# SwiGLU on one core: the first store split over two queues by even and odd partitions, tile 0 computed whole

## The chip, the cores and the metric

The kernel runs on one core of one Trainium2 chip. The metric is the device time of one execution in microseconds (us), as the median of several executions. Five engines work beside each other on a core; this kernel uses ScalarE (ACT in the profile) for the gate, VectorE (DVE) for the product, and SyncE (SP), ScalarE and GpSimd (POOL) to issue transfers. The transfers themselves are carried out by 16 DMA engines, which all three issuing queues share. Two of those queues, SP's and ACT's, are called hardware_dynamic in the profile (q1 and q10), and GpSimd's is called software_dynamic (q0).

## The reference

x is a float32 array of 8192 x 8192. Each row is cut into a left half a and a right half b, and the output is an 8192 x 4096 array:

```
a, b = np.split(x, 2, axis=-1)
silu_b = b / (1 + np.exp(-b))
return a * silu_b
```

So 268.4 MB are read, 134.2 MB are written, and there are two element-wise steps between.

## The kernel before

The 8192 rows are cut into 33 tiles. Tiles 0 and 32 hold 128 rows, one to each of the 128 partitions. Tiles 1 to 31 hold 256 rows, two consecutive rows to each partition. One row of x is 32 KB and one row of the output 16 KB, so a partition's part of a big tile is 64 KB in the load and 32 KB in the store, and in tiles 0 and 32 it is half of that.

There are three buffers in SBUF, slot 0 to 2; tile i lies in slot i % 3. Four things happen to a tile, all in its slot:

- `load(i)` (line 48) issues the load from SP. It waits until the store of tile i - 3, which read the same slot, has landed. Tile 31 (`apart`) is loaded in two halves, one for each row of a partition.
- `swiglu` (lines 57 and 59) runs the gate Silu on ACT in place over b, and then the product on DVE, which writes a * silu(b) packed to the front of the slot. A big tile is one gate and one product. Tile 0 is done in two column halves of 2048 each, two gates and two products, and tile 31 in two halves after its two loads.
- `store(i, engine)` (line 66) issues one store of the whole tile after its last product. The stores of tiles 0 to 29 go out from ACT, but those of tiles 3, 17 and 19 from GpSimd. The stores of tiles 30, 31 and 32 go out from SP.

The order on each engine is the order of the calls in the program (`manual_schedule`): loads 0, 1 and 2 first, and then for each tile gate, product, store and the load of tile i + 3. The instructions of one engine are issued in this order, and a waiting instruction holds up all behind it on its engine. On ACT the store of a tile stands ahead of the gate of the next tile. On SP there are only loads until the last three stores. `behind` records which instruction a new one has to wait for; it takes the list of targets as arguments.

Of the kernel before, what the change touches and what calls it, by code (L numbers as in the profile page):

```python
# [1 line left out]

# [4 lines left out]

_SILU = mybir.ActivationFunctionType.Silu


@with_exitstack
def kernel(
    ctx: ExitStack,
    tc: tile.TileContext,
    x: bass.AP,
    out: bass.AP,
):
    nc = tc.nc
    N, M = x.shape  # L20
    half = M // 2
    P = nc.NUM_PARTITIONS
    rows = [1] + [2] * (N // (2 * P) - 1) + [1]
    first = [P * sum(rows[:i]) for i in range(len(rows))]
    last = len(rows) - 1
    apart = last - 1

    pool = ctx.enter_context(tc.tile_pool(name="sbuf", bufs=1))
    ctx.enter_context(tc.manual_schedule())
    slots = [pool.tile([P, 2 * M], x.dtype, name=f"slot{s}") for s in range(3)]  # L30
    touched = [[] for _ in slots]
    newest = {}
    landed, made, stored = {}, {}, {}

    def behind(inst, s, *targets):
        for t in touched[s]:
            if t not in targets and t is not newest.get(inst.ins.engine):
                tc.declare_no_dep(inst.ins, t.ins, reason="ordered by the other waits")
        touched[s].append(inst)
        newest[inst.ins.engine] = inst  # L40
        return inst

    def load(i):
        s, r = i % 3, rows[i]
        src = x[first[i] : first[i] + P * r].rearrange("(p r) m -> p (r m)", r=r)
        cuts = [0, M, r * M] if i == apart else [0, r * M]
        for c0, c1 in zip(cuts, cuts[1:]):
            inst = nc.sync.dma_start(out=slots[s][:, c0:c1], in_=src[:, c0:c1])  # L48
            behind(inst, s, *([stored[i - 3]] if i >= 3 and c0 == 0 else []))
            landed.setdefault(i, []).append(inst)  # L50

    def swiglu(i, k0, k1, c0, c1):
        s, r = i % 3, rows[i]
        v = slots[s][:, : r * M].rearrange("p (k s c) -> p k s c", k=r, s=2)
        to = slots[s][:, : r * half].rearrange("p (k c) -> p k c", k=r)
        b = v[:, k0:k1, 1, c0:c1]
        gate = nc.scalar.activation(out=b, in_=b, func=_SILU)  # L57
        behind(gate, s, landed[i][min(k0, len(landed[i]) - 1)])
        prod = nc.vector.tensor_mul(out=to[:, k0:k1, c0:c1], in0=v[:, k0:k1, 0, c0:c1], in1=b)  # L59
        behind(prod, s, gate, *([made[i]] if i in made else []))  # L60
        made[i] = prod

    def store(i, engine):
        s, r = i % 3, rows[i]
        dst = out[first[i] : first[i] + P * r].rearrange("(p r) m -> p (r m)", r=r)
        inst = engine.dma_start(out=dst, in_=slots[s][:, : r * half])  # L66
        behind(inst, s, made[i])
        stored[i] = inst

    for i in range(3):  # L70
        load(i)
    for i in range(last + 1):
        if i == 0:
            swiglu(i, 0, 1, 0, half // 2)
            swiglu(i, 0, 1, half // 2, half)
        elif i == apart:
            swiglu(i, 0, 1, 0, half)
            swiglu(i, 1, 2, 0, half)
        else:
            swiglu(i, 0, rows[i], 0, half)  # L80
        if i < last - 2:
            store(i, nc.gpsimd if i in (3, 17, 19) else nc.scalar)
            load(i + 3)
        else:
            store(i, nc.sync)


# [1 line left out]
_INS = ['x']  # L89
_OUTS = [((8192, 4096), 'float32')]  # L90


# [23 lines left out]
```

## Time and profile before

| what | value |
|---|---|
| time, median of 3 runs | 935.28 us (935.13 to 935.88) |
| the profiled execution, its own time | 935.16 us |
| its span in the profile | 933.4 us |
| DVE busy, ACT busy | 278.5 us (30%), 226.7 us (24%) |
| bytes moved by the DMA engines | 402.67 MB, mean 431 GB/s |
| gate of 128x8192, 128x4096, 128x2048, mean | 7029, 3616, 1901 ns |
| product of 128x8192, 128x4096, 128x2048, mean | 8693, 4426, 2288 ns |

The profile describes one execution on the chip. Its page gives the busy time of each engine, the busy share of the DMA engines in slices of the span, the DMA queues with their packets and bytes, the chain of work that ended last, the costliest groups of instructions, and the DMA issues with the median time from issue to landing. The trace behind the page answers further questions: the instructions of a stretch in order of time, the waits, or the busy time and the GB/s of chosen stretches. The 1.76 us between the span (933.4) and the time of that execution (935.16) lie outside of what the profile covers.

### The profile page before, as it was taken

Reading aid. Unit: us, or ns where it says so; the run is one execution under the profiler, and the core shown is the slowest. Engines: PE = TensorE matmul, PEld = TensorE weight load, DVE = VectorE, ACT = ScalarE, POOL = GpSimd, SP = SyncE. Lnnn points to the kernel's source line nnn. Section 1 sums busy time; section 2 is a strip of 40 time slices with the busy share of each in tenths; the row PEclk is TensorE's granted clock in tenths of the full one; section 3 lists DMA queues with packets and bytes.
Section 4 is the critical chain, followed back from the end, with each engine's and each line's share of the span. In section 5 each row is a group of like instructions: output and inputs, shape, how many; then the busy total and the mean of one; then the engine's idle time right before and its main releaser. Section 6 shows DMA issues by size and latency. Waiting matters only on the chain.

```text
span 933.4 us, 211 instructions
## 1 busy us (share of the span) xinstructions
DVE 278.5 (30%) x35; ACT 226.7 (24%) x36; POOL 1.9 (0%) x7
## 2 busy tenths in 40 slices
DVE  1131333123331233312333113332133321333241
ACT  2332033311333203332033320233202333023330
POOL 0000000000000000000000000000000000000000
DMA  9999999999999999999999999999999999999999
GB/s 404 404 458 418 427 452 441 410 445 428 445 427 434 442 411 447 430 435 435 440 420 441 438 424 445 427 454 425 424 452 407 448 427 429 448 441 413 431 438 389
DMA packets 9650, 402.67 MB, mean 431 GB/s; under 512 B 1073, under 2 KB 1073, under 8 KB 1073
## 3 DMA queue, kind: packets, MB, share of 16 engines
q1 hardware_dynamic: 5328, 278.92, 69.1%
q10 hardware_dynamic: 3888, 111.15, 27.6%
q0 software_dynamic: 432, 12.58, 3.1%
q14 instruction: 2, 0.01, 0.0%
HBM read 268.44 MB, written 134.22 MB: 431 GB/s over the span
## 4 chain that ended last, share of the span: by engine, by line
DMA 78%; DVE 11%; ACT 9%; another core or an unknown queue 1%; issue 0%; SPq 0%; ACTq 0%
DMA slot<-in_x_dram 42%; DMA out_dram<-slot 36%; DVE slot L59 11%; ACT slot L57 9%; SPq L48 0%; ACTq L66 0%
## 5 line engine op out<-in xcount | busy, mean ns | idle before, releaser
L59 DVE TENSOR_TENSOR slot<-slot 128x8192 f32<-128x8192 f32 (+2 forms) x35 | 278.5, 7961 | 637.9 <-ACT slot L57 637.9
L57 ACT ACTIVATE slot<-slot 128x8192 f32<-128x8192 f32 (+2 forms) x35 | 225.4, 6444 | 684.5 <-DMA slot<-in_x_dram 684.5
L66 POOL DMA_DIRECT2D out_dram<-slot x3 | 1.7, 578 | 568.7 <-DVE slot L59 568.7
L57 ACT ACT_TABLE_LOAD x1 | 1.3, 1283 | 0.7 <-PEq L100 0.7
L100 POOL MEMSET const-bfloat16-1.0<- 128x1 bf16 x1 | 0.1, 102 | 0.0
L100 POOL MEMSET const-float32-0.0<- 128x1 f32 x1 | 0.1, 99 | 0.2 <-issue 0.2
L100 POOL MEMSET const-float32-1.0<- 128x1 f32 x1 | 0.1, 99 | 0.0
L100 POOL MEMSET const-uint8-127<- 128x1 uint8 x1 | 0.1, 99 | 0.0
## 6 DMA issues: line engine op xcount, KB each, us to landing
out_dram<-slot ACTq DMA_DIRECT2D x26, 4096.0 KB, 33.5
slot<-in_x_dram SPq DMA_DIRECT2D x4, 4096.0 KB, 23.5
out_dram<-slot POOLq DMA_DIRECT2D x3, 4096.0 KB, 34.2
out_dram<-slot SPq DMA_DIRECT2D x2, 4096.0 KB, 25.0
out_dram<-slot ACTq DMA_DIRECT2D x1, 2048.0 KB, 28.1
out_dram<-slot SPq DMA_DIRECT2D x1, 2048.0 KB, 16.1
slot<-in_x_dram SPq DMA_DIRECT2D x30, 37.6
```

The costliest lines, as they stand in the source:

```text
L57: gate = nc.scalar.activation(out=b, in_=b, func=_SILU)
L59: prod = nc.vector.tensor_mul(out=to[:, k0:k1, c0:c1], in0=v[:, k0:k1, 0, c0:c1], in1=b)
L66: inst = engine.dma_start(out=dst, in_=slots[s][:, : r * half])
L100: nc = _bacc.Bacc("TRN2", target_bir_lowering=False, num_devices=1)
```

## The change

Two things are changed. Tile 0 loses its special case: it is gated and multiplied by one instruction each (128x4096) in place of two (128x2048). And `store` takes several engines: with n engines, the tile's partitions are dealt out in turn, so that with two the first engine issues a store of the even partitions and the second one of the odd partitions (64 rows each). Only the store of tile 0 uses this, with ACT for the even and GpSimd for the odd partitions. As a tile can now have two stores, `stored[i]` is a list, and the load of tile 3 waits for both. With one engine, `store` issues the same transfer as before.

```diff
-            behind(inst, s, *([stored[i - 3]] if i >= 3 and c0 == 0 else []))
+            behind(inst, s, *(stored[i - 3] if i >= 3 and c0 == 0 else []))
...
-    def store(i, engine):
-        s, r = i % 3, rows[i]
-        dst = out[first[i] : first[i] + P * r].rearrange("(p r) m -> p (r m)", r=r)
-        inst = engine.dma_start(out=dst, in_=slots[s][:, : r * half])
-        behind(inst, s, made[i])
-        stored[i] = inst
+    def store(i, *engines):
+        s, r, n = i % 3, rows[i], len(engines)
+        dst = out[first[i] : first[i] + P * r].rearrange("(q n r) m -> n q (r m)", n=n, r=r)
+        parts = slots[s][:, : r * half].rearrange("(q n) c -> n q c", n=n)
+        for j, engine in enumerate(engines):
+            inst = engine.dma_start(out=dst[j], in_=parts[j])
+            behind(inst, s, made[i])
+            stored.setdefault(i, []).append(inst)
...
-        if i == 0:
-            swiglu(i, 0, 1, 0, half // 2)
-            swiglu(i, 0, 1, half // 2, half)
-        elif i == apart:
+        if i == apart:
             swiglu(i, 0, 1, 0, half)
             swiglu(i, 1, 2, 0, half)
         else:
             swiglu(i, 0, rows[i], 0, half)
-        if i < last - 2:
+        if i == 0:
+            store(i, nc.scalar, nc.gpsimd)
+            load(i + 3)
+        elif i < last - 2:
             store(i, nc.gpsimd if i in (3, 17, 19) else nc.scalar)
             load(i + 3)
```

On the engines: ACT has one gate in place of two ahead of its first store, and that store has 64 rows in place of 128. DVE has one product in place of two. GpSimd's queue gets a store of 64 rows ahead of its store of tile 3. SP's list is the same, but its fourth load waits for two transfers. Everything after that is unchanged.

## The prediction

> **What bounds the kernel now.** I read the page's engine rows first, then its DMA rows and queues.
>
> ```profile
> span 933.4 us, 211 instructions
> ...
> DVE 278.5 (30%) x35; ACT 226.7 (24%) x36; POOL 1.9 (0%) x7
> ...
> DMA  9999999999999999999999999999999999999999
> ...
> q1 hardware_dynamic: 5328, 278.92, 69.1%
> q10 hardware_dynamic: 3888, 111.15, 27.6%
> q0 software_dynamic: 432, 12.58, 3.1%
> ```
>
> No compute engine is busy a third of the time. The DMA row has a 9 in every slice, and the queues' shares add up to 99.8% of 16 DMA engines over the whole span. So the transfers are the bound. Where could there still be idle time? The table of stretches of 87 us (three tiles each; columns: busy time of DVE, ACT, POOL, clock, DMA share, GB/s) shows it:
>
> ```profile
> 0.00:87.00 87.00, 21.88 (x4) 19.05 (x5) 0.20 (x4) 1.00 0.99 421
> 87.00:174.00 87.00, 26.08 (x3) 21.09 (x3) 0.67 (x1) 1.00 1.00 434
> ...
> 435.00:522.00 87.00, 26.08 (x3) 21.09 (x3) 0.53 (x1) 1.00 1.00 435
> ...
> 870.00:933.40 63.40, 21.97 (x4) 17.88 (x4) 0.00 (x0) 1.00 0.96 413
> ```
>
> All nine stretches between 87 and 870 us stand at 434 or 435 GB/s, with a store from GpSimd in them (three) or without. Against 434, the first stretch lacks 87 x 13/434 = 2.6 us and the last 63.4 x 21/434 = 3.1 us. The first is the start of the first load: issued at 0.74, its 4.19 MB land 12.3 us later where 434 GB/s would need 9.7, so 2.6 us again. Nothing else is left of the first stretch, which is the one that the change edits.
>
> Then the timeline and the chain of waits, for what stands around the first store.
>
> ```profile
> 13.09 3.71 ACT L57 ACTIVATE slot<-slot 128x2048 f32<-128x2048 f32 x2 [11.08 <-DMA slot<-in_x_dram]
> 15.04 4.49 DVE L59 TENSOR_TENSOR slot<-slot 128x2048 f32<-128x2048 f32 x2 [15.04 <-ACT slot L57]
> 19.56 0.38 ACTq L66 DMA_DIRECT2D out_dram<-slot  x1
> 35.63 7.03 ACT L57 ACTIVATE slot<-slot 128x8192 f32<-128x8192 f32 x1 [18.83 <-DMA slot<-in_x_dram]
> 42.69 8.69 DVE L59 TENSOR_TENSOR slot<-slot 128x8192 f32<-128x8192 f32 x1 [23.16 <-ACT slot L57]
> 51.42 0.34 ACTq L66 DMA_DIRECT2D out_dram<-slot  x1
> 58.77 7.03 ACT L57 ACTIVATE slot<-slot 128x8192 f32<-128x8192 f32 x1 [16.11 <-DMA slot<-in_x_dram]
> ```
>
> Gates begin when their loads have landed, so the first three loads land at 13.1, 35.6 and 58.7. The first store is issued at 19.56. The DMA issues put its landing 28.1 us later, and SP issues load 3 at 47.66, which is the same moment.
>
> ```profile
> out_dram<-slot ACTq DMA_DIRECT2D x1, 2048.0 KB, 28.1
> ```
>
> **Why a 2 MB store takes 28.1 us.** The packet counts fit one packet per partition row and 16 small ones per transfer: ACT's 27 stores x (128 + 16) = 3888. So a packet of load 1 or 2 has 64 KB and one of store 0 has 16 KB. If the queues take turns packet by packet, store 0 gets 16/(64 + 16) = 1/5 of 434 GB/s, or 87, and its 2.10 MB take 24.1 us; with the 2.6 us of start and landing from above, 26.7, against 28.1 measured. With equal shares in bytes it would be 12.3. The row decides for turns by packets. [...]
>
> **The change, part by part.**
>
> Tile 0 whole: one gate (3.62) in place of two (3.71), one product (4.43) in place of two (4.49), but now one behind the other. The store is issued at 13.09 + 3.62 + 0.02 + 4.43 + 0.02 = 21.18, which is 1.62 us later than 19.56. ACT's next gate waits for load 1 until beyond 35 and DVE until 42, so nobody on these engines is held up.
>
> Store 0 on two queues: two issues of 64 packets in place of one of 128, at 0.38 us on ACT and 0.67 on GpSimd (its first issue at 103.75, 0.31 us after the product ended; 0.53 later). GpSimd has nothing else before tile 3. If GpSimd's queue has a turn of its own, store 0 gets 32/(64 + 16 + 16) = 1/3 of 434, or 145 GB/s: 14.5 us and 2.6 to 4.0 of start and landing, so it lands at 38 to 40 in place of 47.7, and SP issues load 3 there, once both halves are in.
>
> What that earlier load 3 is worth: nothing, by the order on SP. Load 2 stands ahead of it in the same queue and lands at 58.7. And a share that store 0 gains is one that loads 1 and 2 lose. Load 1: from 13.1 alone until store 0's packets begin (some 2.0 after its issue: 23.2) 4.4 MB, the remaining 4.0 MB at 2/3 of 434 in 13.8 us: 37.0. (The same working for before gives 35.1, the row 35.6.) So load 1 lands near 37.5, 1.9 us later, and store 1 follows at 53.3. Load 2 has the engines almost alone from 38 to 55 and lands near 57.8, 0.9 us earlier.
>
> Is anything late next? Load 4 waits for store 1, issued 1.9 us later, and in before SP issued it at 83.95, when load 3 had 3.7 us to go (87.66). After, it is issued near 85.9, when load 3 has about 0.9 to go. The loads' queue then runs dry for some 2 us, but store 2 (issued near 73.6, 4.19 MB) has the engines meanwhile. What one queue leaves, the other takes; loads 1 and 2 (16.8 MB, 38.7 us) and the stores behind them leave no moment without packets. The 1.6 us is hidden by that, and if that cover were gone it would cost 1.6 at most.
>
> The end: a shift of 1 to 3 us comes to load 32, which waits for store 29 (issued at 885.95, while the loads of tile 31 land until 898.6), and to the last store, issued at 916.4, when store 31, issued at 906.7, has 4.19 MB or 9.7 us to move behind store 30. I estimate 9 us of slack in both places.
>
> The sum: bytes the same, packets the same but 16 more small ones, GpSimd's queue at the same 434 GB/s, idle time the same 2.6 and 3.1 us. One price is not shown by any row: a transfer of every other partition. Each of before uses all 128. At 434/16 = 27.1 GB/s per engine a packet of 16 KB takes 0.605 us, and store 0 has 8 per engine. Between 0 (each engine keeps to its part of SBUF) and each of these packets taking twice as long, +4.8 us; below nothing there is no room, since the engines have no idle time to win. I take 0, since all rows, with loads and stores of 16, 32 and 64 KB packets and one to three queues, stand at 434; both ends go into the range. So 933.4 + 0 in span, 935.16 + 0 in time; beside the median of 935.28 I say **935.3**.
>
> **The rivals.**
>
> [...]
>
> *A shift that opens a gap: slower.* If the phases moved by over 9 us, load 32 or store 32 would come late and the gate and product of the last tile (3.62 + 4.43) would stand open: up to 8 us, 943. My shift is 1 to 3 us.
>
> *The earlier load 3 pays: faster.* It would have to fill idle time of the first stretch, which has 2.6 us, all of it before the first landing. At the very most 935.2 - 2.6 = 932.6.
>
> *The change does not do what it says.* If the second queue gets no turn of its own, store 0 lands near 49 and load 3 is issued there, still ahead of load 2's end: 935.3.
>
> **How the numbers follow.** Hidden by a full queue, at no price: 0.55. No turn of its own, same time: 0.05. Collision: 0.32, of which 0.29 over 0.2% and 0.03 under. A gap: 0.05. The earlier load 3 pays: 0.03. About 0.2% is what a measurement of this kernel can tell from no change. So faster 0.03, same 0.55 + 0.05 + 0.03 = 0.63, slower 0.29 + 0.05 = 0.34. The likeliest case alone would be 934.6 to 936.2; with the collision's full price the range is 934.6 to 940.1.
>
> **What would show it.** Right: one gate and one product for tile 0, store issues near 21.2, both halves landed by 40, load 3 issued there, tile 1's gate near 37.5, tile 2's near 57.8, and 87:870 still at 434. [...] Wrong by a gap: a low rate in the last 30 us alone.

## The result and the profile after

The changed kernel takes 937.89 us (median of 10 runs, 936.73 to 938.37), beside 935.24 us for the kernel before in the same comparison (10 runs). The ratio is 1.0022, with a 95% interval of 1.0012 to 1.0032. It is slower by 0.2%, at the edge of what the prediction counted as no change, and 2.6 us above the 935.3 that the likeliest case gave. Single runs of the kernel before lie above 936 as well, 9 of the 111 in all comparisons of this document. The profiled execution took 937.18 us with a span of 935.4; that is 2.0 us more span than before.

The page and the table of stretches of 87 us of the changed kernel (the same columns as before):

```profile
span 935.4 us, 211 instructions
...
DVE 278.5 (30%) x34; ACT 226.6 (24%) x35; POOL 2.5 (0%) x8
...
q1 hardware_dynamic: 5328, 278.92, 69.1%
q10 hardware_dynamic: 3824, 110.10, 27.3%
q0 software_dynamic: 512, 13.63, 3.4%
```

```profile
0.00:87.00 87.00, 21.81 (x3) 18.96 (x4) 0.84 (x5) 1.00 0.99 418
87.00:174.00 87.00, 26.08 (x3) 21.09 (x3) 0.55 (x1) 1.00 1.02 432
...
522.00:609.00 87.00, 26.08 (x3) 21.09 (x3) 0.53 (x1) 1.00 1.00 434
...
870.00:935.40 65.40, 21.97 (x4) 17.88 (x4) 0.00 (x0) 1.00 0.96 413
```

The sums of work are as before, and so is the end. Look at the second line: the DMA engines are busier (1.02 for 1.00) and move less (432 for 434). From 174 us on the table stands at 434 again, but for 430 between 435 and 522; there the busy share is 0.99, and no packet took longer than usual.

The timeline shows each step of the start:

```profile
13.13 3.62 ACT L57 ACTIVATE slot<-slot 128x4096 f32<-128x4096 f32 x1 [11.11 <-DMA slot<-in_x_dram]
...
21.23 0.56 ACTq L68 DMA_DIRECT2D out_dram<-slot  x1
21.51 0.64 POOL L68 DMA_DIRECT2D out_dram<-slot  x1 [21.07 <-DVE slot L59]
37.37 7.03 ACT L57 ACTIVATE slot<-slot 128x8192 f32<-128x8192 f32 x1 [20.62 <-DMA slot<-in_x_dram]
...
53.16 0.36 ACTq L68 DMA_DIRECT2D out_dram<-slot  x1
58.98 7.03 ACT L57 ACTIVATE slot<-slot 128x8192 f32<-128x8192 f32 x1 [14.58 <-DMA slot<-in_x_dram]
...
88.04 7.03 ACT L57 ACTIVATE slot<-slot 128x8192 f32<-128x8192 f32 x1 [22.04 <-DMA slot<-in_x_dram]
...
122.63 7.03 ACT L57 ACTIVATE slot<-slot 128x8192 f32<-128x8192 f32 x1 [27.56 <-DMA slot<-in_x_dram]
```

Loads 1 and 2 land at 37.4 and 59.0, store 1 goes out at 53.16. The gate of tile 4 starts at 122.63; before it started here:

```profile
119.15 7.03 ACT L57 ACTIVATE slot<-slot 128x8192 f32<-128x8192 f32 x1 [24.44 <-DMA slot<-in_x_dram]
```

And this is when SP issues load 4, first before, then after:

```profile
83.95 0.33 SPq L48 DMA_DIRECT2D slot<-in_x_dram  x1
```

```profile
86.89 0.33 SPq L48 DMA_DIRECT2D slot<-in_x_dram  x1
```

After, the last packet of load 3 ends between 84.5 and 86.5 on the 16 engines, so none of them had a load packet left when load 4 was issued at 86.89. (Load 3 counts as landed on them some 1.5 us later, between 86.1 and 88.0.) The stretch of 90 to 100 us, when load 4's first packets run, first before, then after:

```profile
90.00:100.00 10.00, 5.25 (x1) 4.71 (x1) 0.00 (x0) 1.00 1.09 472
```

```profile
90.00:100.00 10.00, 4.90 (x1) 5.07 (x1) 0.00 (x0) 1.00 1.01 370
```

GB/s by itself jumps in so short a stretch (before: 472 from 90 to 100 us, 410 from 88.5 to 100). GB/s over the DMA share does not: 472/1.09 = 433 and 410/0.95 = 432 before, 370/1.01 = 366 from 90 to 100 us after. Busy engines moved less.

**Where the 2 us lie.** The trace has a record of every packet with its start, its length and its queue. Nearly all packets of a size take the same time in both kernels: 0.611 us for 16 KB, 1.213 for 32 KB, 2.418 for 64 KB. So each packet's extra time can be read off. Summed and divided by 16 engines it is 1.48 us per engine before and 3.33 after, 1.85 more, beside 2.0 of span. Before it is spent at the first packets of the kernel (0.58) and where store 0 joins (20 to 35 us: 0.82). After there are 0.56 and 0.92 in these places, 0.24 between 55 and 85, and 1.58 between 90 and 100, nearly all of it (1.46) on the first or second packet of load 4 on each engine (up to 3.93 us for a packet of 64 KB).

### The profile page after: what moved, and what is told of

It is laid out like the page before. It is cut to its first block, busy times and chain, and to the rows that moved or that the text cites. A ratio compares the mean times of both kernels' runs of the same rounds, so it can differ in the third digit from the quotient of the medians.

```text
span 935.4 us, 211 instructions
## 1 busy us (share of the span) xinstructions
DVE 278.5 (30%) x34; ACT 226.6 (24%) x35; POOL 2.5 (0%) x8
## 4 chain that ended last, share of the span: by engine, by line
DMA 78%; DVE 11%; ACT 9%; another core or an unknown queue 1%; issue 0%; SPq 0%; ACTq 0%
DMA slot<-in_x_dram 42%; DMA out_dram<-slot 35%; DVE slot L59 11%; ACT slot L57 9%; SPq L48 0%; ACTq L68 0%
## 5 line engine op out<-in xcount | busy, mean ns | idle before, releaser
L59 DVE TENSOR_TENSOR slot<-slot 128x8192 f32<-128x8192 f32 (+1 forms) x34 | 278.5, 8190 | 640.0 <-ACT slot L57 640.0
L57 ACT ACTIVATE slot<-slot 128x8192 f32<-128x8192 f32 (+1 forms) x34 | 225.3, 6628 | 686.6 <-DMA slot<-in_x_dram 686.6
## 6 DMA issues: line engine op xcount, KB each, us to landing
out_dram<-slot ACTq DMA_DIRECT2D x1, 1024.0 KB, 19.6
out_dram<-slot POOLq DMA_DIRECT2D x1, 1024.0 KB, 19.4
slot<-in_x_dram SPq DMA_DIRECT2D x30, 37.5
```

## The experiments

All kernels were timed in five rounds against the kernel before, and the ratio is given with its 95% interval. Three theories were written down before the first runs. D: a load that comes into a load queue that has run dry costs. G: the half stores themselves cost. S: the later store costs.

**One part at a time.** `e1` keeps tile 0's two column halves and takes the two-queue store; `e2` takes the whole tile 0 and leaves the store on ScalarE:

```diff
 e1
-        if i == apart:
+        if i == 0:
+            swiglu(i, 0, 1, 0, half // 2)
+            swiglu(i, 0, 1, half // 2, half)
+        elif i == apart:
 e2
-            store(i, nc.scalar, nc.gpsimd)
+            store(i, nc.scalar)
```

> The two-queue store alone; tile 0 stays in two column halves. Theory D (the loss is load 4 coming into a load queue that has run dry, because store 0's larger share delays load 1 and so store 1): load 1 lands near 37.3, SP issues load 4 near 86.8, and the time is 1.5 to 3 us above before. Theory G (the half stores themselves cost: a third queue, or rows two partitions apart): also 1.5 to 3 us above. Theory S (the store that is issued 1.6 us later costs): as before, 935.2.

> Tile 0 whole alone; store 0 goes out from ScalarE in one piece. Theory D: store 0 keeps its fifth, load 1 lands near 35.1, load 4 is issued by 84 and the queue never dries: 935.2 within 0.5. Theory G: 935.2. Theory S: 1.5 to 3 us above before.

Measured: e1 936.84 us, 1.0016 (1.0007 to 1.0025); e2 936.88 us, 1.0017 (1.0008 to 1.0026). Each part alone costs 1.7 us, both together 2.6. e1 went as D and G said: load 1 at 37.84, load 4 issued at 86.40, extra packet time of 1.32 us per engine near 90. e2's time is what S expected (1.5 to 3 us above before) and not what D did; yet D's late load is there: load 1 landed at 37.24, not at 35.1, and load 4 was issued late after all:

```profile
86.65 0.33 SPq L48 DMA_DIRECT2D slot<-in_x_dram  x1
```

But in e2 only 0.23 us per engine was lost there. How a smaller loss gives the same time is answered below.

**The same queue, and load 4 in time.** `e3` issues both half stores from ScalarE; `e4` is the changed kernel with tile 1 in two halves, so that store 1 goes out earlier:

```diff
 e3
-            store(i, nc.scalar, nc.gpsimd)
+            store(i, nc.scalar, nc.scalar)
 e4
-        if i == apart:
+        if i in (1, apart):
```

> Tile 0 whole and the two half stores kept, but both on ScalarE's queue, one after the other. Theory D: one queue, one turn, store 0 keeps its fifth and lands near 49; load 4 is in time: 935.2 to 935.7. Theory G by rows two partitions apart: 1.5 to 3 us above before. Theory G by a third queue: 935.2.

> The changed kernel with tile 1 gated and multiplied in two halves (one row of a partition each), so that its store goes out 3.2 us sooner. Theory D: store 1 near 49.9, load 4 issued near 83.6, before load 3 is through, and the loss is gone: 935.2 to 936. Theory G and theory S: 937 to 938 as the changed kernel.

Measured: e3 935.38 us, 1.0000 (0.9991 to 1.0009); e4 935.30 us, 0.9999 (0.9990 to 1.0007). In both medians the loss is gone. The profile of e3 shows its slowest run, 936.70, where the other ten took 935.29 to 935.60. e3 has the rows two partitions apart, e4 has them and GpSimd's turn besides, so G falls. A later store 0 is not enough for a loss either, since both issue it as late as the changed kernel, so S as it stood falls too, although it had e2 right. e4 issues load 4 at 81.54, e3 (in that run) at 85.38, both before load 3 had landed. So far D fits, if e2's loss is put down to its late load 4.

**Holding back store 1 alone.** Then the kernel before was left as it is, store 0 included, and store 1 was delayed by VectorE instructions that change nothing (the maximum of a piece of the product with itself). One of 128x1024 in `e5`, one of 128x4096 in `e6`, two in `e7`; `e8` has three, ahead of the store of tile 13. This is the edit of `e6`:

```diff
         made[i] = prod
+        if i == 1:
+            for _ in range(1):
+                part = slots[s][:, 0:4096]
+                more = nc.vector.tensor_tensor(out=part, in0=part, in1=part, op=mybir.AluOpType.max)
+                behind(more, s, made[i])
+                made[i] = more
```

> The kernel before, with one more VectorE instruction (128x1024, an element-wise maximum of the product with itself, which leaves it as it is) ahead of store 1, so that store 1 goes out some 1.2 us later and nothing else is changed. Theory D (a load that comes into a dry load queue costs): load 4 issued near 85.2, some 2 us before load 3 is through, so no loss: 935.1 to 935.5. A theory in which each us of delay of store 1 costs a us: 936.3.

> The same with 128x4096, some 4.4 us. Theory D: load 4 issued near 88.4, after load 3 is through at 87.6: the queue is dry, and the stretched load packets of the changed kernel come near 92 although store 0 is as before: 1.3 to 3 us above before. Rival (the loss belongs to what the change does to store 0, and not to the dry queue): 935.2. By the us of delay: 939.6.

> The same with two of 128x4096, some 8.9 us. Theory D with a price for each restart: 1.3 to 3 us above before, as with 4.4 us. Theory D with a price that grows with the time the queue is dry: 4 us or more above. Rival (store 0): 935.2.

> Three of 128x4096 (some 13.3 us) ahead of the store of tile 13, in the middle of the kernel, so that load 16 comes late. Loads there are issued some 8 us before the one ahead of them is through, so the queue runs dry by some 5 us. Theory D: stretched load packets there, 1.3 to 3 us above before. If the loss belongs to the start of the kernel alone: 935.2.

Measured: e5 935.08 us, 1.0006 (0.9998 to 1.0015; three of its 12 runs lie at 936.8 to 938.9, the profiled one among them); e6 936.76 us, 1.0016 (1.0008 to 1.0025); e7 935.30 us, 1.0002 (0.9994 to 1.0011); e8 935.05 us, 0.9999 (0.9990 to 1.0008).

The holds move load 4 by less than themselves: it is issued at 86.34 in e6 and at 86.18 in e7, after holds of 4.4 and 8.9 us, where before it came at 83.95. e6 shows that the loss does not need the change: a late store 1 is enough. But e7 and e8 refute D. In e7 load 3 has landed by 83.8, load 4 is issued at 86.18, and each engine goes 8.5 us without a load packet (7.3 to 8.5 in e6), without any stretched packet near load 4; in e8 the same holds for 9.7 us in the middle of the kernel. In these two a dry queue alone cost 0.2 us at most in the median (935.30 and 935.05 beside 935.10 for the kernel before in that round).

What does differ shows in the packet records. Put end to end (each packet begins where the one before it on its engine ends), they give the sequence of each engine; three engines of each are shown, from 88 us on in the time of the timeline. The records name no engine, so this order is put together, not read. S32 is a store packet of 32 KB, L64 a load packet of 64 KB, with its start, and behind the plus its extra time in ns:

```
e6  S32@89.17  S32@90.38  L64@91.59+303  S32@94.31  L64@95.51+87
    S32@88.10  S32@89.31  L64@90.52+175  S32@93.11  L64@94.32+106
    S32@88.06  S32@89.27  S32@90.48  L64@91.69+538  S32@94.65
e7  S32@89.16  L64@90.37  S32@92.79  L64@94.00
    S32@89.12  L64@90.33  S32@92.75  L64@93.96
    S32@88.12  S32@89.33  L64@90.54  S32@92.95  L64@94.16
```

In e7 all 16 engines take up load 4 at the same turn, between 90.32 and 90.63, and nothing is stretched. In e6 six of them take it up between 90.5 and 90.8 and ten a store packet later, between 91.5 and 91.8, and all 16 are stretched. So a fourth theory, L: **a transfer that joins a running stream may reach the engines across a boundary between turns; then they are split, packets near the split are stretched, and the end of the kernel is set by the slowest engine.**

In ten of the fourteen profiles the records chain so that each engine gets its 240 load packets of 64 KB and its 280 packets of 32 KB; in the other four (the changed kernel, e1, e2 and e6) the chains cross where packets are stretched. In all ten, the span less the largest extra time of one engine is nearly the same, 931.2 to 931.8 us, while the spans run from 933.2 to 937.2 and that extra time from 1.7 to 5.6. (Another way of chaining moves an engine's extra time by some 0.3 us.) This shows where the time is lost; it does not yet show that a split causes it.

The records also answer e2: at 25 us 15 engines took one more load packet before store 0's first, one did not, and it alone lost 2.19 us in this place where the mean is 1.04. It also finished its part of load 1 2.6 us after the first. A gate starts behind the last engine's landing (in the changed kernel load 1 has 16 landings, from 36.27 to 37.34 us, and tile 1's gate starts at 37.37), so in e2 load 1 came late (37.24), hence store 1 (53.03), hence load 4 (86.65), whose start split two more engines off (1.6 and 2.0 us).

**Testing L.** `e9` is e2 with tile 1 in halves, so that load 4 is in time but store 0 joins as in e2; `e10` is the kernel before with the halves alone; `e11` is the changed kernel with e7's hold; `e12` is the kernel before with a hold of 128x4096 and 128x2048.

```diff
 e9, against e2
-        if i == apart:
+        if i in (1, apart):
 e10, against before
-        elif i == apart:
+        elif i in (1, apart):
```

> Tile 0 whole with one store from ScalarE (as in e2), and tile 1 in two halves so that load 4 comes in time. Theory D (a dry load queue costs): the loss of e2 is gone, 935.1 to 935.4. Theory L (a transfer that joins at a turn boundary finds some DMA engines a packet ahead of others; packets near such a split are stretched, and the slowest engine sets the end; a dry load queue only gives the occasion): the dry restart is gone, but store 0 still joins near 21.4 as in e2, where one engine split off, so single runs up to 1.5 us above, the median between 935.1 and 936.3.

> The kernel before with tile 1 in two halves, as a control for e4 and e9: load 4 issued some 3 us earlier than the 83.95 of before. Both theories: 935.0 to 935.3, since there is no dry restart to be saved.

> The changed kernel with two VectorE instructions of 128x4096 ahead of store 1 (8.9 us), so that load 4 joins later still, some 7 us after load 3 is through. Theory D: a dry queue, 937 to 938 as the changed kernel or more. Theory L: it depends on whether the engines take up load 4 at the same turn; if all 16 do, 935.2 to 936 although the queue is dry for longer; if they are split in the trace, 937 or more. By the us of delay: 946.

> The kernel before with 128x4096 and 128x2048 ahead of store 1 (6.7 us), between the 4.4 us that cost 1.7 and the 8.9 us that cost 0.2. Theory D with any price that goes by the length of the delay: between the two, 935.3 to 936.8, for each run. Theory L: a profile with all engines taking load 4 at the same turn has no stretched packets there and 935.1 to 935.4; one with split turns has them and 936 or more; runs of both kinds may occur.

Measured: e9 936.49 us, 1.0014 (1.0005 to 1.0023); e10 935.13 us, 1.0002 (0.9993 to 1.0011); e11 936.28 us, 1.0011 (1.0002 to 1.0020); e12 935.69 us, 1.0004 (0.9995 to 1.0013).

e9 speaks against D. Load 4 is issued long before load 3 is through, no packet near 90 is stretched, and the loss is there:

```profile
81.57 0.33 SPq L48 DMA_DIRECT2D slot<-in_x_dram  x1
91.77 7.03 ACT L57 ACTIVATE slot<-slot 128x8192 f32<-128x8192 f32 x1 [21.97 <-DMA slot<-in_x_dram]
```

Its records show one engine out of step at store 0, as in e2:

```
one of 15    L64@21.85  L64@24.26+374  S16@27.05  L64@27.66+96   S16@30.17  L64@30.78+554
the 16th     L64@22.55+66  S16@25.02   L64@25.63+962  S16@29.01  L64@29.61+498  S16@32.53  L64@33.13+866
```

That engine loses 2.4 us there, the mean 1.16, and with 3.76 us in all it ends the kernel. L's band for the median went to 936.3, and 936.49 lies a little over it; D's 935.4 is far off. e3's profile, of its slowest run, shows the same: one engine loses 2.0 us at store 0, the mean 0.90. e9 and e10 differ in tile 0 alone, and so in a store 0 that is issued at 21.35 in place of 19.45: in a store from ScalarE alone, the later moment cost 1.4 us here (936.49 beside 935.13).

e10 came out as both said. e12's profile has all engines in step (90.35 to 90.89) and took 935.08; of its 11 runs three lie at 935.08 to 935.17 and eight at 935.65 to 936.11, so two kinds of run occur, as L said they may, though only two of the costlier ones reach the 936 that L expected of them; D's 935.3 to 936.8 for each run misses the three. In e11 five engines take load 4 up a turn late and have stretched packets, two of them by over 0.9 us. The loss is half of the changed kernel's, although the queue is dry for longer (9.7 to 12.1 us), and with 936.1 the profiled run stays below the 937 that D and L both expected here.

**What the profiles say together.** This table has load 4 in all fourteen. Where it comes in time, an engine goes 2.4 us (two store packets) without a load packet, as it does at load 5 of the kernel before; where it comes late, longer:

| without a load packet | how the engines take up load 4 | profiles | stretched packets there |
|---|---|---|---|
| 2.4 us | at one turn | before, e4, e8 | none |
| 2.4 us | one engine (e9) or four (e10) are a packet away from the others from earlier on | e9, e10 | none |
| 2.4 to 4.8 us | seven engines after three store packets, eight after four, one out of step from earlier on | e3 | none |
| 8.5 us | at one turn | e7, e12 | none |
| 3.6 to 12.1 us | at different turns | changed kernel, e1, e2, e5, e6, e11 | in all six |

So L is too strong as it stands: in e3 load 4 splits the engines, in e10 they stand apart, and no packet is stretched. Stretched packets at load 4 occur only where the load comes late by this measure and is also taken up at different turns, in six of seven such profiles. It is a count over single profiles, and what sets e3 apart is not known. The profile of e5, its slowest run (938.93), issues load 4 at 87.59 in place of the expected 85.2 and stretches one engine's packets there. Most of its loss lies further on, under the same pair of conditions: load 7, issued at 173.88, finds most engines without a load packet for 4.8 to 8.0 us, they take it up between 177.2 and 179.7, and between 135 and 195 us all 16 lose 0.7 to 2.4 us.

Here is the busy share and GB/s of 90 to 100 us again, of e6 and then of e7: 452/1.08 = 419 against 429/0.99 = 433.

```profile
90.00:100.00 10.00, 7.84 (x1) 2.13 (x1) 0.00 (x0) 1.00 1.08 452
```

```profile
90.00:100.00 10.00, 8.69 (x1) 0.78 (x1) 0.18 (x1) 1.00 0.99 429
```

What stretches a packet near a split is open. The records show where and how long, not what holds it; no run was made for that. In the changed kernel all 16 engines lose 1.2 to 2.0 us near 90, in e2 two alone; why is open too. No kernel beat the kernel before: the lowest ratios are 0.9999 (e4, e8), and their intervals include 1.

## Why the prediction came out as it did

- **The bound** was right: outside of the start nothing but the transfers, 434 GB/s in the undisturbed stretches, the end as before (413 GB/s in the last one), and no time to win.
- **The steps of the start** were right within about 1 us: store issues at 21.2 and 21.5 (forecast 21.18), load 1 at 37.4 (37.5), store 1 at 53.16 (53.3), load 2 at 59.0 (57.8), load 4 issued at 86.89 (85.9); load 2 was the furthest off, 1.2 us. No run shows the 2.0 us that the forecast of load 1 takes from store 0's issue to its first packets; that was the author's estimate, and the records have 4.9 us before (19.56 to 24.44) and 6.2 after (21.23 to 27.46). The halves landed some 19.5 us after their issues, and load 3 followed at 40.96 (38 to 40).
- **The step that failed** is this one: "The loads' queue then runs dry for some 2 us, but store 2 (issued near 73.6, 4.19 MB) has the engines meanwhile. What one queue leaves, the other takes". The queue did run dry, though for longer: each engine went 4.8 to 7.8 us without a load packet, where before it went 2.4. The forecast counted to the landing of load 3 and from the issue of load 4, but in before load 3's last packets end at 85.5 to 86.0, some 1.6 us ahead of its landing, and after the change load 4's first packet starts at 90.5, 3.6 us behind its issue. Store 2 did have the engines, which were busy throughout (a share of 1.04 from 85 to 91 us). But "busy" was taken for "at full rate". Where load 4 joined again, the engines were split and its packets stretched: 1.58 us per engine of the 1.85. The forecast saw the occasion and priced it at 0, at 1.6 at most, because all stretches of before stood at 434; the median rose by 2.65. Before has stretched packets at one joining, store 0's, whose 0.82 us the forecast did not see in stretches of 87 us.
- **The collision** was the wrong rival. No run shows its price, up to 4.8 us for half stores whose packets take twice as long; that was the author's estimate. All 256 packets of 16 KB take 0.611 us in both kernels, those of the half stores included, and the medians of e3 (935.38) and e4 (935.30) have them without loss. The likeliest case alone would have been 934.6 to 936.2, which misses the time. The range reached up to 940.1 by this rival's price, and so it held the time by luck, for a reason that was not the cause.
- **Turns by packets** was right. In total the second queue brought hardly anything (414 GB/s from 20 to 48 us, 412 before), but it gave store 0 a larger share, with a landing 19.4 to 19.6 us after its issues in place of 28.1, and load 1 paid for it (37.4 in place of 35.6). In e3, with both halves on one queue, load 3 was issued only at 53.95.
- **The gap** and **the earlier load 3** did not occur: the end stands as before, and load 3, issued 6.7 us earlier, landed at 88.0 against 87.7.

## What to carry to other kernels

In a kernel that is bound by transfers, divide GB/s by the busy share, stretch by stretch: here the DMA row full of 9s said that the engines were busy, not that they ran at full rate (366 for 433 from 90 to 100 us). Moving a store by little cost more here than it moved: store 0 went out 1.67 us later (21.23 for 19.56), over two queues, and the median rose by 2.65. Store 1 went out late for it (53.16 for 51.42), load 4 was issued late (86.89 for 83.95), and it reached the engines at different turns, with stretched packets (1.58 us per engine). Keep the loads' queue from running dry where it is cheap (e4 got all of the changed kernel's loss back by one tile in halves, 935.30 for 937.89), and time such a change many times: e6 and e7 issue load 4 within 0.2 us of each other (86.34 and 86.18), and one has the loss (936.76) and the other has not (935.30). A profile is one run; those of e3 and e5 are of their slowest.

## What was not expected of the hardware

The start of store 0, 2 MB beside a stream of loads, cost the engines time here: 0.69 to 1.16 us per engine of stretched load packets in all fourteen profiles. In before all 16 engines are in step there, so this cost (0.82 us) is not one of a split. In e9 one engine of 16 that falls behind at 25 us is not made up for to the end; each engine has the same number of packets (240 of 64 KB and 280 of 32 KB), loads 2 to 5 each land with 3.3 us between the first and the last engine, and the span is longer than before's by 1.6 us, where this engine lost some 1.7 us more than the slowest one of before (3.76 against about 2.0). And the price of nearly the same late load goes with one store packet of 1.2 us: 0.2 us over before in e7, where the profile has all engines within 0.32 us, and 1.7 us in e6, where it has them in two groups.
